# A two-layer hybrid encoder on one core: three seven-product pairs per unit, weights split in TensorE's order, gate weights cast by GpSimd

## The chip, the cores and the metric

The kernel runs on one core of a Trainium2 chip, as one launch. The metric is the device time of that launch in microseconds, as the median of several runs. The engines are named as the profile names them: PE is TensorE (matmuls; PEld its weight loads), DVE is VectorE, ACT is ScalarE, POOL is GpSimd, and SP's queue issues the loads from memory. The arithmetic is fp32, but TensorE takes each operand as a high part and a low part (both fp32r), so one product of two fp32 blocks is three matmuls: high by high, high by low, low by high.

## What is computed

256 tokens of width 2048 pass through two layers. Each layer is a token mixer and a gated feed-forward block, both with a residual and an RMS norm ahead:

```python
x = x + mixer(rms_norm(x, norm_mix[i]))
h = rms_norm(x, norm_ffn[i])
x = x + (silu(h @ w_gate) * (h @ w_up)) @ w_down     # 2048 -> 5632 -> 2048
```

Layer 0's mixer is grouped-query attention (16 query heads, 4 key heads of 128, norm and rotation on queries and keys). Layer 1's is a recurrent block: `h @ w_in` gives 2048 x-columns and 2048 gate columns; the x-columns go through a width-4 convolution and two gated linear recurrences, forward and backward, whose gates are block-diagonal products with 256 x 256 blocks; the sum times GeLU of the gate columns goes through `w_out`.

## The kernel before

All weights stream from memory once, in halves of 128 x 1024 fp32 (512 KB). `load_half` issues the load of one half into a buffer `raw`, ScalarE casts it to the high part `hi`, and VectorE subtracts to get the low part `lo`. Each of the three has five buffers. The halves are taken in the order of the list `order`, which is the order in which TensorE uses them. TensorE's own order is the order of the code. On the other engines a scheduler places the instructions by a timeline of its own, within the dependences; `follow(i, j)` adds the rule that i comes after j on its engine.

TensorE's stream also carries the small work of the mixers. `later(delay, fn)` puts a function on a list, `step()` is called between matmuls and counts, and when the count is reached the function is run at that place. `USUAL` and `LATE` give the delays of one attention head: the sums of squares, the scores, the turning of the probabilities, the values, and the split of the rotated query (`qs`). `WHEN` gives those of one block of the recurrence: four gates, four decays, four scans, GeLU, two finishes. In the projections of the recurrence a step is one `three`, that is three 256-wide matmuls; in attention's, one 512-wide and one 256-wide.

The feed-forward block works on units of 4 x 128 hidden columns, eleven in a layer. For one unit, the 16 contraction tiles are taken as 8 pairs. A pair holds two tiles of the gate weights and two of the up weights. Four accumulators (c11, c21, c12, c22: gate and up for each half of the tokens) take a plain pair as 8 products (`wide`). For the pairs named in `SEVEN` a Strassen-like form needs 7 products: `Norm.form` makes four sums of activations (`forms`) once per layer, `load_seven` makes four sums of the weights (t1 to t4) and splits them too, and four products go to banks of their own (m1, p5, p7, p6), which `unit` adds up at the end of the last such pair (lines 692 to 697). At a unit's end VectorE empties the four accumulators (L700, L703), the result is turned, split and kept as `act` tiles.

`PARTS` says after how many hidden tiles their share of `w_down` is multiplied: after the first unit of the next part come four down groups (512 output columns each) of the part before, all in a row. Each ends in `add_residual`. Accumulators are PSUM banks: four `acc` (`new_acc`) and four `pm`; before, down groups use `acc`.

## Time and profile before

| what | value |
|---|---|
| median of 3 runs | 2016.78 us (2014.33 to 2016.87) |
| profiled execution, its own time | 2015.84 us |
| its span, first to last instruction | 2013.9 us |
| mean granted TensorE clock | 0.997 |
| busy: PE / DVE / ACT / POOL | 1996.0 / 1527.1 / 1283.5 / 226.1 us |
| memory read | 382.13 MB, 191 GB/s over the span |
| attention | up to about 190 us, its output projection to 275 us |
| feed-forward of layer 0 | 275 to 978 us |
| recurrence | 978 to about 1230 us, its output projection to 1307 us |
| feed-forward of layer 1 | 1307 us to the end |

A row of the groups view names line, engine, operation, output and inputs by the program's tile names, shape and count, then busy time, mean ns of one, and the idle time of the engine just before with what ended it. A timeline row gives start, duration, engine, line, tiles and how many instructions were merged. A row of stretches gives, for each engine, the busy time and the number of instructions, then the granted clock, the DMA share and GB/s. The matmul time of one instruction is its latency; matmuls overlap, so pace is read from starts.

### The profile page before, as it was taken

Reading aid. Unit: us, or ns where it says so; the run is one execution under the profiler, and the core shown is the slowest. Engines: PE = TensorE matmul, PEld = TensorE weight load, DVE = VectorE, ACT = ScalarE, POOL = GpSimd, SP = SyncE. Lnnn points to the kernel's source line nnn. Section 1 sums busy time; section 2 is a strip of 40 time slices with the busy share of each in tenths; the row PEclk is TensorE's granted clock in tenths of the full one; section 3 lists DMA queues with packets and bytes.
Section 4 is the critical chain, followed back from the end, with each engine's and each line's share of the span. In section 5 each row is a group of like instructions: output and inputs, shape, how many; then the busy total and the mean of one; then the engine's idle time right before and its main releaser. Section 6 shows DMA issues by size and latency. Waiting matters only on the chain.

```text
span 2013.9 us, 27692 instructions
## 1 busy us (share of the span) xinstructions
PE 1996.0 (99%) x9994; PEld 1701.5 (84%) x9994; DVE 1527.1 (76%) x1982; ACT 1283.5 (64%) x1985; POOL 226.1 (11%) x305
## 2 busy tenths in 40 slices
PE   9999999999999999999899999999999999999999
PEld 8888888888888888888799998888888888888887
DVE  7888698886568865686768886898886578856764
ACT  7566676666346674467688987867665456654562
POOL 0454220000000000001333330400000000000000
PEclk9999999999999999999999999999999999999999
DMA  8444565655656656665656555565666556666654
GB/s 315 151 130 138 184 200 190 211 197 185 212 182 208 200 185 212 196 200 187 198 158 189 181 176 178 188 202 185 211 207 196 189 188 197 213 198 197 199 180 156
DMA packets 108569, 386.04 MB, mean 192 GB/s; under 512 B 12176, under 2 KB 12432, under 8 KB 108304
## 3 DMA queue, kind: packets, MB, share of 16 engines
q1 hardware_dynamic: 108288, 384.26, 59.0%
q8 instruction: 78, 1.28, 0.2%
q14 instruction: 59, 0.48, 0.1%
q10 hardware_dynamic: 144, 0.02, 0.0%
HBM read 382.13 MB, written 2.10 MB: 191 GB/s over the span
## 4 chain that ended last, share of the span: by engine, by line
PE 92%; DVE 4%; POOL 2%; issue 1%; DMA 1%; ACT 0%; SPq 0%; POOLq 0%; DVEq 0%; ACTq 0%
PE acc L261 24%; PE acc L258 24%; PE acc L259 24%; PE acc L238 3%; PE acc L239 3%; PE acc L240 3%; PE pm L259 2%; PE pm L258 2%; PE pm L261 2%; PE acc L227 2%; DVE lo L111 1%; POOL hb L508 1%; PE pm L240 1%; PE pm L239 1%; PE acc L225 1%
## 5 line engine op out<-in xcount | busy, mean ns | idle before, releaser
L111 DVE TENSOR_TENSOR lo<-raw,hi 128x1024 fp32r<-128x1024 f32 (+1 forms) x617 | 754.4, 1235 | 364.2 <-ACT hi L110 358.9
L110 ACT CAST hi<-raw 128x1024 fp32r<-128x1024 f32 (+1 forms) x617 | 639.3, 1049 | 535.1 <-PE acc L259 496.7
L258 PE MATMUL acc<-hi,xg 128*128 128x512 f32 x1100 | 427.9, 389 | 0.0
L259 PE MATMUL acc<-hi,xg 128*128 128x512 f32 x1100 | 427.9, 389 | 0.0
L261 PE MATMUL acc<-lo,xg 128*128 128x512 f32 x1100 | 427.9, 389 | 0.0
L258 PE MATMUL acc<-hi,act 128*128 128x512 f32 x960 | 373.9, 389 | 0.0
L261 PE MATMUL acc<-lo,act 128*128 128x512 f32 x960 | 373.5, 389 | 0.0
L259 PE MATMUL acc<-hi,act 128*128 128x512 f32 x960 | 373.5, 389 | 0.0
L258 PEld LDWEIGHTS acc<-hi,xg 128*128 128x128 f32 x1100 | 206.5, 188 | 42.9
L261 PEld LDWEIGHTS acc<-lo,xg 128*128 128x128 f32 x1100 | 206.5, 188 | 42.9
L259 PEld LDWEIGHTS acc<-hi,xg 128*128 128x128 f32 x1100 | 206.5, 188 | 42.9
L261 PEld LDWEIGHTS acc<-lo,act 128*128 128x128 f32 x960 | 180.2, 188 | 37.5
L259 PEld LDWEIGHTS acc<-hi,act 128*128 128x128 f32 x960 | 180.2, 188 | 37.4
L258 PEld LDWEIGHTS acc<-hi,act 128*128 128x128 f32 x960 | 180.2, 188 | 36.8
L348 ACT COPY hid<-turned 32x256 f32<-32x256 f32 x436 | 175.9, 404 | 10.2 <-DVE turned L341 5.3
L348 POOL COPY hid<-turned 32x256 f32<-32x256 f32 x84 | 58.3, 694 | 801.8 <-DVE turned L341 731.0
L239 PE MATMUL acc<-xg,hi 128*128 128x256 f32 x512 | 146.0, 285 | 1.4 <-DVE xg L363 1.4
L238 PE MATMUL acc<-xg,hi 128*128 128x256 f32 x512 | 146.3, 286 | 0.0
L240 PE MATMUL acc<-xg,lo 128*128 128x256 f32 x512 | 145.6, 284 | 0.0
L227 PE MATMUL acc<-xg,hi 128*128 128x512 f32 x384 | 125.9, 401 | 1.5 <-DVE xg L363 1.5
L131 ACT CAST wsh<-ws 128x1024 fp32r<-128x1024 f32 x88 | 92.2, 1050 | 43.3 <-DVE ws L126 43.2
L132 DVE TENSOR_TENSOR wsl<-ws,wsh 128x1024 fp32r<-128x1024 f32 x88 | 107.7, 1226 | 0.0
(216 smaller groups left out, 2655.3 us busy)
## 6 DMA issues: line engine op xcount, KB each, us to landing
raw<-in_w_gate_dram SPq DMA_DIRECT2D x176, 512.0 KB, 3.9
raw<-in_w_up_dram SPq DMA_DIRECT2D x176, 512.0 KB, 4.1
raw<-in_w_down_dram SPq DMA_DIRECT2D x176, 512.0 KB, 4.3
raw<-in_w_in_dram SPq DMA_DIRECT2D x64, 512.0 KB, 4.3
raw<-in_w_qv_dram SPq DMA_DIRECT2D x40, 512.0 KB, 4.0
raw<-in_w_o_dram SPq DMA_DIRECT2D x32, 512.0 KB, 3.5
raw<-in_w_out_dram SPq DMA_DIRECT2D x32, 512.0 KB, 3.6
graw<-in_w_gates_dram SPq DMA_DIRECT2D x32, 256.0 KB, 3.5
```

Source lines behind the costliest of these rows:

```text
L110: newest["cast"] = act.copy(hi[:, sl], raw[:, sl])
L111: dve.tensor_tensor(lo[:, sl], raw[:, sl], hi[:, sl].bitcast(F32), ALU.subtract)
L131: act.copy(hs[:, sl, :], sums[:, sl, :])
L132: dve.tensor_tensor(ls[:, sl, :], sums[:, sl, :], hs[:, sl, :].bitcast(F32), ALU.subtract)
L227: pe.matmul(acc, w, xs[k], start=(k == 0), stop=stop)
L238: pe.matmul(o, hi, x[:, :S], start=start, stop=False)
L239: pe.matmul(o, hi, x[:, S:], start=False, stop=False)
L240: pe.matmul(o, lo, x[:, :S], start=False, stop=stop)
L258: pe.matmul(o, xh, wh, start=start, stop=False)
L259: pe.matmul(o, xl, wh, start=False, stop=False)
L261: pe.matmul(o, xh, wl, start=False, stop=stop)
L348: (eng.copy if eng is act else eng.tensor_copy)(to[:, :, :, i, :], of[:, :, :, j, :])
```

## The change

1. `SEVEN` has three pairs (0, 3, 5) for nine of the eleven units; units 1 and 2 keep two (0, 5). The seven products are issued in another order: those with plain weights first.
2. `load_seven` casts, sums and splits in the order of the products, and `behind` ties each cast on ScalarE, and each sum or subtraction on VectorE, behind the last one of its kind. So weights are split in the order in which TensorE uses them, everywhere.
3. `parts` gives the split weights of the feed-forward parts two more buffers for `hi` and `lo` (seven in all); the sums of weights use buffers of the same ring.
4. `PARTS` is 8, 8, 8, 8, 12: after each unit from the third to the tenth come two down groups (`ffn_plan`), which now use the `pm` banks. `act` tiles have four buffers.
5. At the start of the recurrence `held` puts the casts from the fifth weight half on behind the last tile of the norm (`xg`), and the first block's gates come later (`WHEN_FIRST`).
6. In attention the first six heads' scores come later (`EARLY`), the last head's by three steps; VectorE scales the probabilities in place of GpSimd.
7. The gate weights are cast by GpSimd instead of ScalarE, from four raw buffers instead of two.

```diff
-PARTS = [16, 16, 12]
+PARTS = [8, 8, 8, 8, 12]
-SEVEN = (0, 4)
+SEVEN = (0, 3, 5)
+FEWER = (0, 5)
+FEW = (1, 2)
+RING = 5
+MORE = 2
-LATE = ((10, 23, 15, 13, 9), (5, 15, 17, 9, 5))
+EARLY = (32, 31, 30, 28, 26, 24)
+LATE = ((10, 23, 15, 13, 9), (5, 18, 17, 9, 5))
 WHEN = (18, 25, 32, 39, 42, 46, 50, 54, 58, 60, 62, 64, 66, 70, 74)
+WHEN_FIRST = (28, 34, 40, 46, 49, 53, 57, 60, 62, 64, 66, 68, 70, 74, 78)
...
+    def parts(shape):
+        n = ring[0] = (ring[0] + 1) % (RING + MORE)
+        if ft and n >= RING:
+            return [scope[-1].tile(shape, F32R, tag="x" + t, name=nm(t), bufs=MORE) for t in ("hi", "lo")]
+        return [wp.tile(shape, F32R, tag=t, name=nm(t), bufs=RING) for t in ("hi", "lo")]
+
+    def behind(key, i):
+        if key in newest:
+            follow(i, newest[key])
+        newest[key] = i
...
     def load_half(src, pieces=1, then=None):
...
-            newest["cast"] = act.copy(hi[:, sl], raw[:, sl])
-            dve.tensor_tensor(lo[:, sl], raw[:, sl], hi[:, sl].bitcast(F32), ALU.subtract)
+            behind("cast", act.copy(hi[:, sl], raw[:, sl]))
+            behind("rest", dve.tensor_tensor(lo[:, sl], raw[:, sl], hi[:, sl].bitcast(F32), ALU.subtract))
+        for rule in held:
+            rule[0] -= 1
+            if rule[0] < 0:
+                follow(newest[rule[1]], rule[2])
...
     def load_seven(srcs):
...
+        def two(src, names):
+            hi, lo = parts([P, 2, WIDE]) if len(names) > 1 else [tmp(t, (P, 1, WIDE), F32R) for t in ("ohi", "olo")]
+            behind("cast", act.copy(hi, src))
+            for j, name in enumerate(names):
+                got[name] = hi[:, j, :], lo[:, j, :]
+            return lambda: behind("rest", dve.tensor_tensor(lo, src, hi[:].bitcast(F32), ALU.subtract))
+
+        def add(o, x, y):
+            behind("rest", dve.tensor_tensor(o, x, y, ALU.add))
+
+        sums = [tmp("ws", (P, 2, WIDE)) for _ in range(2)]
+        (t1, t3), (t2, t4) = ([t[:, j, :] for j in range(2)] for t in sums)
+        two(raw[0], ("b11", "b21"))()
+        add(t1, b11, b12)
+        add(t3, b12, b22)
+        two(raw[1][:, 1:, :], ("b22",))()
+        first = two(sums[0], ("t1", "t3"))
+        add(t2, t1, b22)
+        add(t4, t2, b21)
+        second = two(sums[1], ("t2", "t4"))
+        first()
+        second()
...
+    def ffn_plan():
+        at = np.cumsum([0] + PARTS) // UNIT
+        plan = [("unit", i) for i in range(at[1])]
+        for p in range(len(PARTS) - 1):
+            for n, i in enumerate(range(at[p + 1], at[p + 2])):
+                plan.append(("unit", i))
+                plan += [("down", (p, g)) for g in range(2 * n, min(2 * n + 2, NW))]
+        return plan
...
+            if g == NW - 1 and self.g[0] == "norm_mix":
+                held.extend([[4, "cast", newest["xh"]], [4, "rest", newest["xl"]]])
...
+        if h < len(EARLY):
+            d_sc = EARLY[h]
...
-                eng.tensor_scalar(pr[:, a, :], pr[:, a, :], rs[:, a : a + 1], 1.0, ALU.mult, ALU.mult)
+                dve.tensor_scalar(pr[:, a, :], pr[:, a, :], rs[:, a : a + 1], None, ALU.mult)
...
-                for o, x, y in ((m1, a11, "b11"), (p5, n1, "t1"), (p7, n3, "t3"), (p6, n2, "t2")):
-                    product(o, x, wt[y], first, end)
-                for o, x, y in ((c21, a22, "t4"), (c11, a12, "b21"), (c12, n4, "b22")):
-                    product(o, x, wt[y], first, False)
+                for o, x, y in (
+                    (m1, a11, "b11"), (c11, a12, "b21"), (c12, n4, "b22"), (p5, n1, "t1"),
+                    (p7, n3, "t3"), (p6, n2, "t2"), (c21, a22, "t4"),
+                ):
+                    product(o, x, wt[y], first, end and any(o is m for m in (m1, p5, p7, p6)))
...
+                add_residual(i[1], wide_project(hid[i[0]], PARTS[i[0]], bank), None)
...
-        raw = tmp("graw", (P, 4, P), bufs=2)
+        raw = tmp("graw", (P, 4, P), bufs=GATE_BUFS)
...
-        act.copy(hi, raw)
+        pool.tensor_copy(hi, raw)
...
+        if b > 0:
+            held.clear()
...
-            when = WHEN if nxt else WHEN_LAST
+            when = WHEN_LAST if not nxt else WHEN if b else WHEN_FIRST
```

What this does to the order, at three places. First VectorE at the end of unit 0 of layer 0, before (e0 and e2 take accumulators c11 and c21, `hid` takes c12 and c22; the numbers are the tiles'):

```order
L128 TENSOR_TENSOR lo_748_3588<-raw_744_3584,hi_746_3586 128x512
L111 TENSOR_TENSOR lo_754_3629<-raw_752_3627,hi_753_3628 128x1024
L700 TENSOR_TENSOR e0_710_3428<-e0_710_3428,acc_670_3228 128x512
L700 TENSOR_TENSOR e2_712_3430<-e2_712_3430,acc_671_3229 128x512
L111 TENSOR_TENSOR lo_757_3647<-raw_755_3645,hi_756_3646 128x1024
L703 TENSOR_TENSOR hid_732_3545<-acc_672_3230,e1_711_3429 128x512
L703 TENSOR_TENSOR hid_732_3545<-acc_673_3231,e3_713_3431 128x512
```

and now, with the split of the next unit's first seven-product pair ahead of it (lo_764 to lo_770):

```order
L129 TENSOR_TENSOR lo_773_3661<-raw_771_3659,hi_772_3660 128x1024
L129 TENSOR_TENSOR lo_776_3679<-raw_774_3677,hi_775_3678 128x1024
L741 TENSOR_TENSOR e0_732_3493<-e0_732_3493,acc_674_3240 128x512
L741 TENSOR_TENSOR e2_734_3495<-e2_734_3495,acc_675_3241 128x512
L129 TENSOR_TENSOR lo_779_3697<-raw_777_3695,hi_778_3696 128x1024
L744 TENSOR_TENSOR hid_748_3574<-acc_676_3242,e1_733_3494 128x512
L744 TENSOR_TENSOR hid_748_3574<-acc_677_3243,e3_735_3496 128x512
```

One weight subtraction stands between the pairs of accumulators in both; now two more wide ones stand ahead of the first.

Second, VectorE where layer 0 ends and the recurrence begins, before (x is the residual, `hid` the turned copy, `xg` the scaled tiles of the norm):

```order
L282 TENSOR_TENSOR x_75<-x_75,acc_1717_8711 128x512
L111 TENSOR_TENSOR lo_1765_8946<-raw_1763_8944,hi_1764_8945 128x1024
L282 TENSOR_TENSOR x_75<-x_75,acc_1718_8712 128x512
L111 TENSOR_TENSOR lo_1790_9057<-raw_1788_9055,hi_1789_9056 128x1024
L341 STREAM_TRANSPOSE turned_1742_8837<-x_75 128x1024
L403 TENSOR_REDUCE nm_1739_8827<-ssq_665_3223 128x2
L348 COPY hid_1743_8838<-turned_1742_8837 32x8x32 x2
L408 TENSOR_SCALAR nm_1739_8827<-nm_1739_8827 128x2
L348 COPY hid_1743_8838<-turned_1742_8837 32x8x32 x6
L111 TENSOR_TENSOR lo_1793_9087<-raw_1791_9085,hi_1792_9086 128x1024
L111 TENSOR_TENSOR lo_1800_9130<-raw_1798_9128,hi_1799_9129 128x1024
```

and now:

```order
L129 TENSOR_TENSOR lo_1905_9155<-raw_1903_9153,hi_1904_9154 128x1024
L318 TENSOR_TENSOR x_75<-x_75,acc_1857_8920 128x512
L318 TENSOR_TENSOR x_75<-x_75,acc_1858_8921 128x512
L377 STREAM_TRANSPOSE turned_1882_9046<-x_75 128x1024
L443 TENSOR_REDUCE nm_1879_9036<-ssq_669_3235 128x2
L384 COPY hid_1883_9047<-turned_1882_9046 32x8x32 x2
L448 TENSOR_SCALAR nm_1879_9036<-nm_1879_9036 128x2
L384 COPY hid_1883_9047<-turned_1882_9046 32x8x32 x6
L466 TENSOR_TENSOR rsq_s_1881_9040<-nm_1879_9036,nr_1880_9039 128x2
```

The four weight subtractions between the residual and the norm's last tiles moved ahead of the residual or behind the tiles.

Third, VectorE after the first head's query is split in attention, before (hv is the mean square, mx the maximum of the scores, qs the split query) and now:

```order
L585 SCALAR_TENSOR_TENSOR hv2_159_855<-ms_139_758,ebt_104 128x2
L588 TENSOR_REDUCE mx_162_864<-pm_158_848 128x2
L313 CAST qs_151_822<-hq_149_816 128x256
L426 TENSOR_TENSOR rsq_s_161_858<-hv2_159_855,hf2_160_857 128x2
L314 TENSOR_TENSOR qs_151_822<-hq_149_816,qs_151_822 128x256
```

```order
L627 SCALAR_TENSOR_TENSOR hv2_162_883<-ms_139_758,ebt_104 128x2
L129 TENSOR_TENSOR lo_204_1042<-raw_202_1040,hi_203_1041 128x1024
L349 CAST qs_151_822<-hq_149_816 128x256
L466 TENSOR_TENSOR rsq_s_164_886<-hv2_162_883,hf2_163_885 128x2
L350 TENSOR_TENSOR qs_151_822<-hq_149_816,qs_151_822 128x256
L345 TENSOR_TENSOR hy_169_903<-acc_153_824,hy_169_903 128x256
L467 SCALAR_TENSOR_TENSOR rsq_s_164_886<-rsq_s_164_886,hf2_163_885 128x2
L630 TENSOR_REDUCE mx_165_892<-pm_161_876 128x2
```

The maximum of head 0's scores moved behind a weight subtraction and head 1's query.

## The prediction

> **What bounds the kernel now.** I read the page's busy row first, then the waits of TensorE, then stretches around each wait, and last the queues of the engines that feed it.

> ```profile
> PE 1996.0 (99%) x9994; PEld 1701.5 (84%) x9994; DVE 1527.1 (76%) x1982; ACT 1283.5 (64%) x1985; POOL 226.1 (11%) x305
> ```

> TensorE is busy for all but 18 us of the span. A busy PE need not be at full pace, so the pace comes from starts. Here are the first matmuls of the second unit of layer 0, with what VectorE did beside them:

> ```profile
> 317.36 0.39 PE L258 MATMUL pm<-hi,xg 128*128 128x512 f32 x1
> 317.59 0.39 PE L259 MATMUL pm<-hi,xg 128*128 128x512 f32 x1
> 317.59 1.21 DVE L111 TENSOR_TENSOR lo<-raw,hi 128x1024 fp32r<-128x1024 f32 x1
> ...
> 318.72 0.68 DVE L703 TENSOR_TENSOR hid<-acc,e 128x512 f32<-128x512 f32 x1
> ```

> The next unit begins at 359.52, 186 matmuls later: 42.16 / 186 = 0.2267 us for each 512-wide matmul. In the feed-forward parts (190 to 975 us, and from 1230) the waits of TensorE show nothing. All waits over 0.5 us lie in the mixers (columns: total us, times, longest):

> ```profile
> PE pm L240 <- DVE qs L314: 3.6, 2, 2.8
> PE pm L238 <- DVE xs L313: 2.8, 2, 1.7
> PE acc L227 <- DVE xg L363: 1.5, 1, 1.5
> PE pm L604 <- POOL pr L598: 1.5, 1, 1.5
> PE acc L239 <- DVE xg L363: 1.4, 1, 1.4
> ...
> PE pm L239 <- DVE xs L314: 1.0, 1, 1.0
> PE pm L416 <- POOL cb L739: 0.7, 1, 0.7
> ```

> (The xg wait of 1.5 is the start of the program and stays.) Stretches around them, the clock in the column after POOL:

> ```profile
> core 0: us, PE busy (x) PEld busy (x) DVE busy (x) ACT busy (x) POOL busy (x), PEclk, DMA share, GB/s
> 69.20:72.30 3.10, 0.28 (x3) 0.07 (x1) 3.10 (x5) 0.14 (x2) 2.83 (x3) 1.00 0.17 69
> 72.30:75.80 3.50, 3.49 (x13) 3.11 (x14) 3.21 (x10) 1.45 (x3) 1.34 (x2) 0.58 0.50 150
> 100.00:190.00 90.00, 89.26 (x562) 79.25 (x562) 80.31 (x177) 58.92 (x165) 49.94 (x63) 1.00 0.43 134
> 317.36:359.52 42.16, 42.16 (x187) 34.91 (x186) 37.27 (x43) 29.38 (x42) 0.00 (x0) 1.00 0.64 219
> 986.80:991.00 4.20, 2.10 (x13) 1.47 (x12) 3.75 (x11) 1.51 (x4) 0.23 (x4) 1.00 0.61 178
> 991.00:994.50 3.50, 3.50 (x19) 3.50 (x18) 1.38 (x2) 1.42 (x2) 0.00 (x0) 0.51 0.73 235
> 1001.10:1007.20 6.10, 2.15 (x9) 1.24 (x8) 6.05 (x11) 2.13 (x3) 3.06 (x4) 0.79 0.83 256
> 1007.20:1011.20 4.00, 4.00 (x20) 4.00 (x20) 1.20 (x3) 2.38 (x4) 1.52 (x3) 0.50 0.43 131
> 1020.00:1230.00 210.00, 210.00 (x1720) 208.26 (x1720) 171.02 (x282) 188.73 (x321) 74.11 (x93) 1.00 0.56 172
> ```

> A wait is followed here by about 3.5 to 4 us at half clock, so it costs twice. In all three places VectorE is the full engine. So: fewer matmuls pay in full while VectorE keeps up, and the waits in the mixers are a second, separate reserve.

> **Part 1, matmuls.** A seven-product pair replaces 8 products by 7, three matmuls each. Nine of eleven units per layer get a third pair (units 1 and 2 keep two): 18 pairs, 54 matmuls, 54 x 0.2267 = 12.2 us.

> **Part 2, what VectorE and ScalarE pay.**

> ```profile
> L131 ACT CAST wsh<-ws 128x1024 fp32r<-128x1024 f32 x88 | 92.2, 1050 | 43.3 <-DVE ws L126 43.2
> ...
> L126 DVE TENSOR_TENSOR ws<-ws,raw 128x512 f32<-128x512 f32 x88 | 60.8, 691 | 0.6
> ```

> ```profile
> 304.83 0.69 DVE L126 TENSOR_TENSOR ws<-raw,raw 128x512 f32<-128x512 f32 x1 [3.42 <-DMA raw<-in_w_up_dram]
> ...
> 308.38 2.35 DVE L111 TENSOR_TENSOR lo<-raw,hi 128x1024 fp32r<-128x1024 f32 x2
> ```

> Back to back, a 1024-wide subtraction takes 1.14 us (2.35 - 1.21), a 512-wide one about 0.61 (0.69 less the same 0.08 of overlap). A plain pair costs VectorE two wide subtractions; a seven-product pair three wide ones, one narrow and four sums: 4.2 us more. A two-pair unit keeps VectorE busy for 37.27 of 42.16 us, so one with three needs 41.5, against 183 x 0.2267 = 41.5 for TensorE. Alone that is no slack at all. But the new order puts two down groups (48 matmuls, 10.9 us, each; VectorE 4 x 1.14 + 2 x 0.65 = 5.9) after every unit from the third to the tenth: 53.3 of 63.3 us. Only unit 0 and the last have three pairs without them, and unit 0's successor has two. ScalarE gets two casts more per pair (about 1.6 us net on 29.38). Cost on the path: none, covered by this slack and by seven buffers of split weights instead of five; the 3.42 us that VectorE idled before a sum, for a DMA, also show room. Nothing more is loaded, and the loads keep TensorE's order on SP's queue, five deep as before; there the cover is the lead of the splitting over TensorE. The forms of the third pair (one set per layer, on ScalarE, GpSimd and VectorE) are made while the output projection's last group still runs. Four tiles for the hidden values instead of five cost nothing: the fifth unit writes over the first one's, whose last reader, the fourth down group, stands before it.

> The new product order does add a wait: bank c12 is written after two products (1.36 us) instead of six (4.1 us). VectorE empties it behind one weight subtraction, as the order still has it. In the rows above that ended at 318.72 + 0.68 = 319.40, 2.04 us into the unit: 0.7 us late. Units 0 to 1 and 1 to 2 follow directly in each layer; from the third on a down group stands between and uses the other banks. In before the later boundaries emptied the bank in time, so I charge one per layer, 1.4 us. Ends: 0, and 2 x (0.7 + 4.2 + half of 3.5 at half clock) = 13.

> **Part 3, attention.**

> ```profile
> 69.08 0.28 PE L238 MATMUL pm<-kv,qs 128*128 128x256 f32 x1
> ...
> 71.31 0.94 DVE L314 TENSOR_TENSOR qs<-hq,qs 128x256 fp32r<-128x256 f32 x1
> ...
> 73.05 0.69 DVE L585 SCALAR_TENSOR_TENSOR hv<-ms,ebt 128x2 f32<-128x2 f32 x1
> ```

> ```profile
> L598 POOL TENSOR_SCALAR pr<-pr,rs x30: 480/482/493, 78.4 to 190.8; 128x256 f32<-128x256 f32 x30
> ...
> L598 DVE TENSOR_SCALAR pr<-pr,rs x2: 349/351/353, 195.1 to 195.3; 128x256 f32<-128x256 f32 x2
> ```

> Head 0's scores come 10 steps later; a step is one 512 and one 256-wide matmul, 0.35 us, so they start at 72.6, when qs is ready (72.25). That wait and its slow clock go: 2.8 + 3.5 x 0.42 = 4.3 us. The wait of 1.5 for the scaled probabilities (1.8 with its tail) goes, since GpSimd no longer scales them behind the rotations; the last head's 0.7 goes with three steps more. Together 6.8. Given back: VectorE's queue now has a weight subtraction and head 1's query split ahead of head 0's maximum, and a second subtraction behind it. From 73.05 that queue, both exponentials and the scaling add up to about 8.1 us, to 81.2; TensorE wants the turn 17 steps and a set of scores after 73.3, at 80.1. Take 1.1 lost. Later heads: VectorE was busy for 80.31 of 90 us in 100 to 190 (the stretches above), and 11 heads with 0.7 us more make 88, so this cover is thin; it holds since GpSimd, 1 us freer per head, slows VectorE less. Net 5.7; ends 2 (the wait turns into as long a one) and 6.8.

> **Part 4, start of the recurrence.**

> ```profile
> 978.32 0.28 PE L238 MATMUL acc<-xg,hi 128*128 128x256 f32 x1
> 978.44 0.28 PE L239 MATMUL acc<-xg,hi 128*128 128x256 f32 x1
> ...
> 981.32 1.24 DVE L341 STREAM_TRANSPOSE turned<-x 128x1024 f32<-128x1024 f32 x1
> ...
> 985.83 2.36 DVE L111 TENSOR_TENSOR lo<-raw,hi 128x1024 fp32r<-128x1024 f32 x2
> ...
> 988.37 0.48 DVE L363 SCALAR_TENSOR_TENSOR xg<-hid,pk,xg 128x256 fp32r<-128x256 f32 x1
> ```

> What is lost: 986.8 to 991, 4.2 less 13 matmuls of 0.12, 2.7; then 3.5 x 0.49 = 1.7; 1001.1 to 1007.2, 6.1 less 9 x 0.12, 5.0; then 2.0. Together 11.4. The new rule holds the casts from the fifth weight half on behind the last xg. In the new order two weight subtractions no longer stand between the residual and its transpose, nor two between the copies and xg: about 1.5 + 2.3 us earlier, so the last xg come near 984.5 to 986.2, and the thirteenth is wanted at 987: 4.4 gone. The first gates come 10 steps of three matmuls (3.6 us) later, but counted from an earlier point. VectorE's conv work now stands between weight subtractions that wait for buffers TensorE frees. The last of them needs one freed 20.6 us after 978.3; with cast (1.05), subtraction (1.14) and the split behind (0.43) that is 23.4, and TensorE wants it at 22.5. So about 0.9 stays of 7.0. Net 10.5; ends 4.4 (as late as now) and 11.4.

> **Part 5, gate weights on GpSimd.**

> ```profile
> L770 POOL TENSOR_TENSOR glo<-graw,ghi 128x512 fp32r<-128x512 f32 x32 | 49.4, 1544 | 37.5 <-ACT ghi L769 37.5
> ...
> L769 ACT CAST ghi<-graw 128x512 fp32r<-128x512 f32 x32 | 19.6, 612 | 17.3 <-PE pm L239 10.0 <-DMA graw<-in_w_gates_dram 6.0 <-PE acc L239 1.4
> ```

> ```profile
> 69.33 2.64 POOL L508 TENSOR_TENSOR hb<-hy,rope 64x256 f32<-64x256 f32 x2 [1.08 <-DVE hy L309]
> ```

> ScalarE loses 19.6 us in a stage where it is busy for 188.73 of 210. GpSimd gets 32 casts; no row has that cast, the nearest (482 ns for 256 wide) gives 0.96 us, the subtraction at 1.54 an upper end: 31 to 49 us, room beside 74.11 of 210. The gate loads stay on SP's queue behind weight loads; with four raw buffers instead of two they wait less. Behind a cast that waits for a DMA stand GpSimd's products for the scans, due only at the block's end. Cost on the path 0; from -1 (a freer ScalarE) to +5.
> VectorE and GpSimd slow each other: at 69.65 a subtraction took 1.74 us beside GpSimd's 2.64. [...]

> **Sum.** -12.2 + 1.4 - 5.7 - 10.5 + 0 = -27.0. The profiled execution took 2015.84 (span 2013.9 and 1.9 around it), so 1988.8; the median of the runs is 0.94 higher: 1989.7, say 1990.

> **Rivals.**
> 1. The mixers' waits only move: matmuls fall, but conv and scores stay late, since VectorE was busy for all of 69.2 to 72.3 and 6.05 of 6.10 us at 1001. Net 12.2 - 1.4 + 2 + 4.4 = 17, so 2000; with nothing from the mixers, 2006. For it: full VectorE. Against: the order frees it just ahead of xg, and more steps are given. Chance 0.15.
> 2. GpSimd holds VectorE: 31 us more in the recurrence, 171 to about 199 of 210; seven blocks each 4 us later could show as 1 us of wait and its slow clock at each, about 14 us: 2004. Against: it still fits. Chance 0.07.
> 3. Slower: a three-pair unit makes TensorE wait at its start, for its third and fourth bank (the second down group's sums stand behind weight subtractions) or for weights. Decides from 27 / 18 = 1.5 us per unit; at 1.4 us of wait and 1.5 of slow clock, 18 x 2.9 = 52: 2042. Against: that bank is wanted 3.4 us into the unit and freed about 1.9 in. Chance 0.05. [...]
> 4. My forecast, 1985 to 1997: 0.70. Else (a small gain or none): 0.03.

> **Range.** All gains in full: 12.2 + 6.8 + 11.4 = 30.4, 1986 against the median; I put 1985. The upper end, 2003, takes in most of rival 1 and 2. Faster by over 0.2% (4 us, about what these runs can tell from none) 0.92, within 0.02, slower 0.06.

> **What would show it.** PE records fewer by 54 and a unit of 41.5 us; no PE wait in the feed-forward over 1 us, except on c12 at two unit boundaries; the waits on xg and qs gone, one near 80 us on pr, one near 1001 on xs below 2 us; no stretch at half clock after 20 us or one short one. Wrong would be: half clock at unit starts, VectorE over 95% in 1020 to 1230 with PE idle, or the xs wait as long as before.

## The result, and the profile after

The changed kernel takes 2000.99 us (median of 4 runs, 1999.41 to 2001.07) against 2016.78 before (4 runs): ratio 0.9923, 95% interval 0.9906 to 0.994. The gain is 15.8 us where 27 were forecast. The time lies in the range that the prediction stated, 1985 to 2003, but outside the likeliest case's own range (1985 to 1997), and 1 us from the 2000 that the first rival gave. The profiled execution took 2001.05 us, its span is 1999.3, 14.6 shorter than before.

The busy row of the page:

```profile
PE 1981.1 (99%) x9940; PEld 1686.6 (84%) x9940; DVE 1629.9 (82%) x2154; ACT 1297.6 (65%) x1995; POOL 256.4 (13%) x315
```

TensorE has exactly 54 records fewer (9994 to 9940) and is busy for 14.9 us less; VectorE gained 102.8 us of work. The waits of TensorE, longest sums first:

```profile
PE pm L275 <- DVE pT L649: 3.6, 7, 0.9
PE pm L646 <- DVE pr L640: 2.5, 5, 0.9
PE acc L263 <- DVE xg L399: 1.9, 1, 1.9
PE acc L294 <- DVE e L741: 1.4, 2, 1.1
PE pm L275 <- DVE xs L350: 1.3, 2, 0.9
PE pm L274 <- DVE xs L349: 1.0, 1, 1.0
```

The waits of before on qs (2.8) and on xg in the recurrence (1.4) are gone. In their place stand twelve small ones in the attention: seven on pT, which is the transposed probabilities' low half that VectorE writes, and five on pr, which VectorE now scales. To see what each stage won, take the first matmul of each from the timeline of TensorE (start, duration, line, form); of after first, then of before (whose recurrence begins at 978.32, in a row of the prediction):

```profile
48.94 0.27 PE L590 MATMUL pm<-ident,hy 128*128 128x128 f32 x1
277.73 0.39 PE L294 MATMUL pm<-hi,xg 128*128 128x512 f32 x1
976.79 0.28 PE L274 MATMUL acc<-xg,hi 128*128 128x256 f32 x1
1296.65 0.39 PE L294 MATMUL pm<-hi,xg 128*128 128x512 f32 x1
```

```profile
47.43 0.28 PE L550 MATMUL pm<-ident,hy 128*128 128x128 f32 x1
275.20 0.39 PE L258 MATMUL pm<-hi,xg 128*128 128x512 f32 x1
...
1306.91 0.39 PE L258 MATMUL pm<-hi,xg 128*128 128x512 f32 x1
```

The differences of these starts are the lengths of the stages; the last stage ends with TensorE's last matmul, at 2010.19 before and 1995.54 after.

| stage | before | after | change | predicted |
|---|---|---|---|---|
| program's start, to the first turned head | 47.43 | 48.94 | +1.5 | 0 |
| attention, to the first feed-forward unit | 227.77 | 228.79 | +1.0 | -5.7 |
| feed-forward 0 | 703.12 | 699.06 | -4.1 | -5.4 |
| recurrence and its output projection | 328.59 | 319.86 | -8.7 | -10.5 |
| feed-forward 1 | 703.28 | 698.89 | -4.4 | -5.4 |
| sum | | | -14.7 | -27.0 |

Four places miss their sum, the attention by more than half of it. Stretches of after (columns as in the prediction; the clock stands after POOL), the first at the program's start:

```profile
7.00:10.50 3.50, 3.50 (x12) 3.07 (x13) 3.04 (x6) 3.30 (x8) 0.00 (x0) 0.54 1.03 416
100.00:190.00 90.00, 86.15 (x540) 75.63 (x539) 82.82 (x193) 55.24 (x159) 39.33 (x40) 1.00 0.39 124
1020.00:1230.00 210.00, 210.00 (x1679) 206.48 (x1679) 179.07 (x295) 178.49 (x293) 98.60 (x110) 1.00 0.56 173
```

In 100 to 190 TensorE was busy for 89.26 of 90 us before and is for 86.15 now, while VectorE went from 80.31 to 82.82, although the program advanced less in that time (540 matmuls instead of 562). The start's 1.5 us is no part of the change: TensorE's first wait, 1.9 us here and 1.5 in before, is followed here by a stretch at clock 0.54, and in a second profile of the same kernel (c1, below) by none.

What the attention's small waits look like, on three engines in order of time (rows are left out at the dots); a row's bracket gives the idle time before it and its releaser:

```profile
125.49 0.68 DVE L649 TENSOR_TENSOR pT<-pm,pT 128x512 fp32r<-128x512 f32 x1
...
126.23 0.39 PE L275 MATMUL pm<-pT,kv 128*128 128x256 f32 x1 [0.88 <-DVE pT L649]
...
126.72 2.41 POOL L548 TENSOR_TENSOR hb<-hy,rope 64x256 f32<-64x256 f32 x2 [3.01 <-DVE hf L468]
126.76 1.78 DVE L129 TENSOR_TENSOR lo<-raw,hi 128x1024 fp32r<-128x1024 f32 x1
...
129.21 0.73 POOL L549 TENSOR_TENSOR hq<-hy,rope 128x256 f32<-128x256 f32 x1
129.41 1.48 DVE L640 TENSOR_SCALAR pr<-pr,rs 128x256 f32<-128x256 f32 x2
130.23 0.30 PE L646 MATMUL pm<-ident,pr 128*128 128x128 f32 x1 [0.71 <-DVE pr L640]
```

VectorE goes from one instruction to the next with hardly a pause, in the rows left out too. The two scalings, 0.35 us each in the median of all 32, take 1.48 together here, beside GpSimd's products for hq. TensorE waits for pT and for pr because VectorE reaches them late.

### The profile page after: what moved, and what is told of

Its sections match the earlier page's. It is cut to its first block, busy times and chain, and to the rows that moved or that the text cites. A ratio compares the mean times of both kernels' runs of the same rounds, so it can differ in the third digit from the quotient of the medians.

```text
span 1999.3 us, 27804 instructions
## 1 busy us (share of the span) xinstructions
PE 1981.1 (99%) x9940; PEld 1686.6 (84%) x9940; DVE 1629.9 (82%) x2154; ACT 1297.6 (65%) x1995; POOL 256.4 (13%) x315
## 4 chain that ended last, share of the span: by engine, by line
PE 87%; DVE 7%; POOL 2%; issue 1%; ACT 1%; DMA 1%; SPq 0%; DVEq 0%; ACTq 0%; POOLq 0%
PE acc L294 16%; PE acc L295 16%; PE acc L297 16%; PE pm L297 8%; PE pm L295 8%; PE pm L294 8%; PE acc L274 3%; PE acc L275 3%; PE acc L276 3%; DVE lo L129 2%; PE acc L263 1%; POOL hb L548 1%; PE pm L275 1%; PE pm L276 1%; PE pm L274 1%
## 5 line engine op out<-in xcount | busy, mean ns | idle before, releaser
L129 DVE TENSOR_TENSOR lo<-raw,hi 128x1024 fp32r<-128x1024 f32 (+1 forms) x581 | 712.0, 1242 | 170.2 <-ACT hi L128 167.0
L128 ACT CAST hi<-raw 128x1024 fp32r<-128x1024 f32 (+1 forms) x581 | 596.6, 1048 | 299.1 <-PE acc L295 227.5
L294 PE MATMUL acc<-hi,xg 128*128 128x512 f32 x1036 | 403.3, 389 | 1.8 <-DVE e L741 1.4
L297 PE MATMUL acc<-lo,xg 128*128 128x512 f32 x1036 | 403.0, 389 | 0.0
L295 PE MATMUL acc<-hi,xg 128*128 128x512 f32 x1036 | 403.0, 389 | 0.0
L146 ACT CAST hi<-ws 128x1024 fp32r<-128x1024 f32 x124 | 130.6, 1054 | 194.5 <-DVE ws L152 192.3
L294 PEld LDWEIGHTS acc<-hi,xg 128*128 128x128 f32 x1036 | 194.5, 188 | 43.2 <-DVE e L741 2.3
L294 PE MATMUL pm<-hi,act 128*128 128x512 f32 x512 | 199.2, 389 | 0.0
L295 PE MATMUL pm<-hi,act 128*128 128x512 f32 x512 | 199.2, 389 | 0.0
L297 PE MATMUL pm<-lo,act 128*128 128x512 f32 x512 | 199.2, 389 | 0.0
L384 ACT COPY hid<-turned 32x256 f32<-32x256 f32 x436 | 175.9, 404 | 23.9 <-DVE turned L377 14.7
L294 PE MATMUL acc<-hi,act 128*128 128x512 f32 x448 | 174.6, 390 | 0.0
L297 PE MATMUL acc<-lo,act 128*128 128x512 f32 x448 | 174.4, 389 | 0.0
L295 PE MATMUL acc<-hi,act 128*128 128x512 f32 x448 | 174.3, 389 | 0.0
L149 DVE TENSOR_TENSOR lo<-ws,hi 128x1024 fp32r<-128x1024 f32 x124 | 151.8, 1225 | 6.4 <-ACT hi L146 3.6
```

The costliest lines, as they stand in the source:

```text
L128: behind("cast", act.copy(hi[:, sl], raw[:, sl]))
L129: behind("rest", dve.tensor_tensor(lo[:, sl], raw[:, sl], hi[:, sl].bitcast(F32), ALU.subtract))
L146: behind("cast", act.copy(hi, src))
L149: return lambda: behind("rest", dve.tensor_tensor(lo, src, hi[:].bitcast(F32), ALU.subtract))
L294: pe.matmul(o, xh, wh, start=start, stop=False)
L295: pe.matmul(o, xl, wh, start=False, stop=False)
```

## The experiments

Each is an edit of the changed kernel. Two profiles of the changed kernel agree in each stage to 0.2 us, but for the start with its clock (the changed kernel again, below); times of one kernel spread over 0.5 to 5.5 us, so stages are read first. No run takes away the two additional buffers, the new `PARTS` or the order of the splits alone, so what each of these is worth by itself is not shown.

**Scaling back on GpSimd.**

```diff
-                dve.tensor_scalar(pr[:, a, :], pr[:, a, :], rs[:, a : a + 1], None, ALU.mult)
+                eng.tensor_scalar(pr[:, a, :], pr[:, a, :], rs[:, a : a + 1], 1.0, ALU.mult, ALU.mult)
```

> The changed kernel with one line undone: GpSimd scales the probabilities again, the scores keep their new steps. In the changed kernel TensorE loses 0.35 to 1.1 us at nearly every head between 80 and 195 us, mostly on pT and pr from VectorE. Theory (VectorE is full there because of the 0.7 us of scaling per head): the small waits on pT go, the part from 100 us to the first feed-forward matmul (277.73) shortens by 3 to 4 us, the wait for pr near 80 is about 1 us longer since GpSimd scales behind the next head's rotation; in all 1997 to 1999. Rival (the earlier places of the first six scores crowd VectorE, not the scaling): the waits on pT stay, 2000 to 2002.

Measured: 1996.95 us (ratio to before 0.9903, 0.989 to 0.9917). The attention takes 225.59 us instead of 228.79: 3.2 less. Its stretch and its waits from 75 to 200 us:

```profile
100.00:190.00 90.00, 88.43 (x554) 77.98 (x554) 77.07 (x175) 58.17 (x165) 50.87 (x64) 1.00 0.41 133
```

```profile
PE pm L646 <- POOL pr L640: 2.7, 3, 1.1
PE pm L275 <- DVE pT L649: 1.1, 3, 0.5
```

VectorE falls from 82.82 to 77.07 us, TensorE gains 2.3, the waits on pT fall from 3.6 to 1.1, and the wait for pr near 80 grows, as the theory had it. The time holds more than the edit: in this profile the start is without half clock (1.00 from 7.00 to 10.50 us; 1.6 us less), and the start of the recurrence has one (0.50 from 997.30 to 1000.30 us; 2.7 us more).

**Scaling on ScalarE.**

```diff
-                dve.tensor_scalar(pr[:, a, :], pr[:, a, :], rs[:, a : a + 1], None, ALU.mult)
+                act.activation(pr[:, a, :], pr[:, a, :], AF.Copy, scale=rs[:, a : a + 1])
```

> The changed kernel with the probabilities scaled by ScalarE (a copy with a scale, two of about 0.35 us per head), which is busy for 51 of 84 us there. Theory (VectorE is full because of the scaling): the waits on pT go, 3 to 5 us: 1996 to 1998. Rival (it is the chain of a head, not VectorE's load, or ScalarE's queue now stands behind the reciprocal and its weight casts come late): 2000 or more.

Measured: 1998.38 us (0.9911, 0.9897 to 0.9924); attention 226.19 us, 2.6 less. Whichever engine takes the scaling away from VectorE, the waits on pT shrink (here to 2.0). So it is VectorE's load, not the chain through GpSimd. ScalarE's copy takes 0.50 us, not the 0.35 that the expectation set.

**Steps of before for the scores.**

```diff
-EARLY = (32, 31, 30, 28, 26, 24)
+EARLY = ()
-LATE = ((10, 23, 15, 13, 9), (5, 18, 17, 9, 5))
+LATE = ((10, 23, 15, 13, 9), (5, 15, 17, 9, 5))
```

> The changed kernel with the steps of all scores as before (the first six heads again at 22, the last at 15); VectorE still scales the probabilities. Theory (VectorE is full because of the scaling): the waits on pT per head stay, and the wait of 2.8 us on qs with its half clock comes back, 4.3 us: first feed-forward matmul at 281 to 282, 2005. Rival (the new steps crowd VectorE): the waits per head go and only the qs wait comes back: feed-forward at 277 to 278, 2000 to 2001.

Measured: 2003.86 us (0.9934, 0.9921 to 0.9948); attention 230.62 us, 1.8 more than in the changed kernel. The wait of 2.8 on qs is back, but this time no half clock follows it:

```profile
72.30:75.80 3.50, 2.08 (x13) 1.91 (x14) 3.50 (x7) 0.58 (x3) 2.68 (x3) 1.00 0.42 140
```

The waits on pT fall from 3.6 to 2.4. Both theories have a part: the new steps remove a wait of 2.8 us, and crowd VectorE a little more. They are worth 1.8 us here, not the 4.3 of the prediction; the 1.5 us of half clock that followed this wait in before would come on top.

**The seven products in the old order.**

```diff
-                    (m1, a11, "b11"), (c11, a12, "b21"), (c12, n4, "b22"), (p5, n1, "t1"),
-                    (p7, n3, "t3"), (p6, n2, "t2"), (c21, a22, "t4"),
+                    (m1, a11, "b11"), (p5, n1, "t1"), (p7, n3, "t3"), (p6, n2, "t2"),
+                    (c21, a22, "t4"), (c11, a12, "b21"), (c12, n4, "b22"),
```

> The changed kernel with the seven products in the order of before (all four PSUM banks of the mixed products first, then c21, c11, c12). In the changed kernel TensorE waits at the second unit of each layer, 1.3 and 1.5 us, for bank c11, which the second product writes and VectorE still empties behind two weight subtractions. Theory (the early use of c11 alone makes these waits): both go, unit 0 to unit 1 without a gap, 2.8 us less: 1998. Rival (VectorE is behind at this place, and whatever comes second waits): the gap stays near 1 us, on another bank or on a weight, 2000 to 2001.

Measured: 2018.68 us (1.001, 1.0001 to 1.0019). Both theories fall: all that the change gained is gone again. The waits at 320 and 1339 are gone too, but each of the eight units that follow two down groups, in either layer, has a wait of 1.03 us; the feed-forward stages take 708.06 and 707.70 us. Its rows, in one of these units, which begins at 426.57:

```profile
428.47 0.40 PE L297 MATMUL pm<-lo,fh 128*128 128x512 f32 x1
428.90 0.68 DVE L318 TENSOR_TENSOR x<-x,pm 128x512 f32<-128x512 f32 x1
429.73 0.47 PE L294 MATMUL pm<-hi,fh 128*128 128x512 f32 x1 [0.86 <-DVE x L318]
```

The fourth product wants the bank that the second down group used, and VectorE adds that bank to the residual only at 428.90, behind weight subtractions. (At 11 of these 16 units the profile names a cast on ScalarE that ends as late, in its place. That cast is of a later pair's weights, and the addition stands there too, ending 0.15 us ahead of TensorE's start in all 16.) In the changed kernel the same bank is wanted sixth:

```profile
427.35 0.39 PE L294 MATMUL pm<-hi,xg 128*128 128x512 f32 x1
429.70 0.68 DVE L318 TENSOR_TENSOR x<-x,pm 128x512 f32<-128x512 f32 x1
430.75 0.39 PE L294 MATMUL pm<-hi,fh 128*128 128x512 f32 x1
```

It is free 3.0 us into the unit (430.38 less 427.35) and wanted at 3.4.

**The new order everywhere but in the second unit.**

```diff
+                if direct and first:
+                    prods = tuple(prods[j] for j in (0, 3, 4, 5, 1, 2, 6))
...
-                hid[int(np.searchsorted(ends, i, "right"))] += unit(FEWER if i in FEW else SEVEN)
+                hid[int(np.searchsorted(ends, i, "right"))] += unit(FEWER if i in FEW else SEVEN, i == 1)
```

> The changed kernel with the first pair of unit 1 alone in another order (the four PSUM banks of the mixed products first, then c11, c12, c21); all other units as changed. Theory (c11 is wanted too early only where a unit follows another at once, the other banks only where a down group stands between): the waits of 1.2 to 1.3 us at 320 and of 1.5 at 1339 go and nothing comes in their place: both feed-forward stages 1.3 to 1.5 us shorter, 1998.2. Rival (in unit 1 the weights of the mixed products come late, as in the kernel with this order everywhere): a wait of about 1 us in the first 4 us of unit 1, 2000 to 2001.

Measured: feed-forward 697.91 and 697.83 us, 1.15 and 1.06 less; the waits named e are gone. That is the theory, a little under its size: in layer 1 a wait of 0.4 us on the next accumulator (`hid`) comes in their place. The time is 2001.32 (0.9918, 0.9905 to 0.9932), no better, since here 2.7 us went at the start of the recurrence, after the same waits on xs as in the changed kernel: there the clock fell this time (0.50 from 1000.30 to 1003.30 us).

**Three pairs in every unit.**

```diff
-FEW = (1, 2)
+FEW = ()
```

> The changed kernel with three seven-product pairs in units 1 and 2 too: 4 pairs and 12 matmuls fewer, 2.7 us if VectorE keeps up. These two units follow each other with no down group between, where the prediction reckoned 41.5 us of VectorE work in 41.5 us: no slack. Theory (the lead of seven buffers and the down groups carry it): feed-forward stages 1.3 to 1.4 us shorter each (697.7 and 697.5), 1998.3. Rival (without slack a unit starts late): a new wait of 1 us or more at the start of unit 2 or 3 in each layer, on a bank or a weight, 2001 to 2004.

Measured: 2004.58 us (0.9938, 0.9926 to 0.9951). Twelve matmuls less, and the feed-forward stages are longer, 700.62 and 699.79. The rival holds in its main point, that without slack TensorE waits, but most of the wait is elsewhere. At the start of the third unit of each layer the third product waits 0.9 us for an accumulator. Twice as much, 1.9 us with its tails, is lost in the middle of that unit; in layer 0:

```profile
374.40 6.64 ACT L384 COPY hid<-turned 32x256 f32<-32x256 f32 x16 [0.62 <-DVE turned L377]
381.06 1.04 ACT L146 CAST hi<-ws 128x1024 fp32r<-128x1024 f32 x1
382.14 1.22 DVE L149 TENSOR_TENSOR lo<-ws,hi 128x1024 fp32r<-128x1024 f32 x1 [5.34 <-ACT hi L146]
382.16 0.50 PE L294 MATMUL pm<-hi,fh 128*128 128x512 f32 x1 [0.84 <-ACT hi L146]
```

The sums' cast stands on ScalarE behind 16 copies of the transposed hidden values; VectorE idles for 5.34 us.

**Start of the recurrence as before.**

```diff
-                held.extend([[4, "cast", newest["xh"]], [4, "rest", newest["xl"]]])
+                pass
...
-            when = WHEN_LAST if not nxt else WHEN if b else WHEN_FIRST
+            when = WHEN_LAST if not nxt else WHEN
```

> The changed kernel without the rule that holds the casts behind the last xg, and with the gates at their old steps: what the prediction counted as 10.5 us of gain in the recurrence and the profile shows as 8.7. Theory (both together made it): the waits on xg near 10 us into the recurrence and on xs near 25 us into it come back with their half clock; the stage is 328 to 329 us again and the time 2009 to 2010. Rival (the order of weights made by ScalarE and VectorE, or freed ScalarE, made much of it): 2003 to 2006.

Measured: 2006.12 us (0.9948, 0.9935 to 0.996); the stage takes 326.19 us, 6.3 more than in the changed kernel and 2.4 less than before.

```profile
PE pm L274 <- DVE xs L349: 3.2, 2, 2.9
PE pm L275 <- DVE xs L350: 1.5, 1, 1.5
PE pm L456 <- POOL cb L777: 0.8, 1, 0.8
PE acc L275 <- DVE xg L399: 0.7, 1, 0.7
```

So both rules make most of the 8.7, in between the two expectations; the rest goes to the order in which VectorE and ScalarE now make the weights, which alone halves the wait on xg (1.4 before). Part of the 6.3 is clock: 6.8 us at half clock lie among and behind the waits on xs in this profile, and none in the changed kernel's.

**Without the rule that holds the casts**, the first of those two edits alone.

> The changed kernel without the rule that holds the casts, the first block's gates at their new, later steps. Theory (the two halves are separate): the waits on xg come back, 2.7 us and some 1.7 of half clock, the waits on xs stay as in the changed kernel: 2004 to 2006. Rival (VectorE's work is only moved to the place where xs is made): the xg waits come back and the xs waits go, 2001.

Measured: 2002.40 us (0.993, 0.9917 to 0.9942), stage 322.80. The waits on xg and cb are back (0.7 and 0.8), those on xs fall to one of 1.8. Neither expectation is met whole. Most of what the rule saves at xg, VectorE loses at xs; of its own worth, 2.9 us in these two profiles, about half can be clock: here 3.4 us at half clock follow the wait on xs, in the changed kernel none (below). The later gates, 326.19 less 322.80, are worth 3.4.

**Later gates.**

```diff
-WHEN_FIRST = (28, 34, 40, 46, 49, 53, 57, 60, 62, 64, 66, 68, 70, 74, 78)
+WHEN_FIRST = (36, 40, 44, 48, 51, 53, 57, 60, 62, 64, 66, 68, 70, 74, 78)
```

> The changed kernel with the first recurrence block's four gate steps at 36, 40, 44, 48 instead of 28, 34, 40, 46. In the changed kernel TensorE waits there on xs for 1.2, 0.65 and 1.0 us, and in four of the other profiles a stretch at half clock follows. Theory (the gates stand too early by about 3 us, eight steps): the xs waits fall below 0.5 us in sum, no half clock, the stretch from the first recurrence matmul to the second feed-forward is 317 us (319.9 in the changed kernel's profile, up to 323.6 in the others): 1997 to 1998. Rival (VectorE is behind there as a whole and the wait moves to later work of the block): a new wait of 2 us or more between 1003 and 1020, 2000 to 2001.

Measured: 1998.97 us (0.9906, 0.9893 to 0.992), stage 318.18, 1.7 less. One wait on xs is left, 0.9 us, and no other came; nearer to the theory, short of its 317.

**Gate weights cast by ScalarE.**

```diff
-        pool.tensor_copy(hi, raw)
+        act.copy(hi, raw)
```

> The changed kernel with the 32 gate-weight casts on ScalarE again. Theory (they lie beside TensorE's work on either engine): the recurrence keeps its length, TensorE has no wait in 1020 to 1230, 2000 to 2001. Rival (GpSimd's casts hold VectorE up): VectorE's busy time in 1020 to 1230 falls by 10 us or more and the start of the recurrence loses less, 1998.

Measured: 1999.14 us (0.9912, 0.9899 to 0.9926), stage 319.31; its start was one without half clock (1.00 from 7.00 to 10.50 us), which is 1.6 of the 1.9 us to the changed kernel.

```profile
1020.00:1230.00 210.00, 210.00 (x1671) 206.10 (x1670) 175.83 (x290) 189.34 (x316) 69.06 (x86) 1.00 0.56 173
```

TensorE is busy throughout in both kernels. With the casts GpSimd is busy for 29.5 us more in this stretch (98.60 less 69.06), and VectorE for 3.2, a tenth of that, with five instructions more (295 and 290).

**The changed kernel again.**

> The changed kernel itself once more, for what differs between two profiles of the same program. Theory (a wait of about 2 us switches the clock, and small differences of the loads decide it): the program's first wait is again between 1.1 and 2.3 us, with 3 us of half clock behind it only if it exceeds 2.0, worth 1.5 us; the waits on xs are 2.8 to 4.5 us again, with or without half clock. Rival (the kernel always has a slow start): half clock from 7 to 11 us whatever the wait.

Measured: 2001.26 us (0.9923, 0.9909 to 0.9937). Stages as in the first profile to 0.2 us, but for the start: 47.98 instead of 48.94 for the first turned head, no half clock behind a first wait that ended 1.85 us after the last matmul's start, against 2.17. The rival is out.

**Combined.** Four edits: GpSimd scales; the first head's turn seven steps later; the second unit's order; later gates.

> The changed kernel with four edits: GpSimd scales the probabilities, the first head's turn stands 7 steps later (24 instead of 17), unit 1 starts in the other product order, the first block's gates stand later. Theory (the four waits are separate): 3.2 us from the scaling, up to 2.5 from the first turn, 2.8 from the two units, 2.8 from the gates: 1990 to 1992, where the prediction had put the change itself. Rival (VectorE's work in the mixers only comes late at the next place): 1995 or more.

Measured: 1993.33 us (0.988, 0.9867 to 0.9894), the fastest kernel here, some 8 us under the changed one. Attention 225.48, feed-forward 698.29 and 697.85, recurrence 318.23. Scaling, second unit and gates keep most of their gains. The later turn gave nothing (225.59 without it): the wait for pr was only moved.

```profile
PE pm L648 <- POOL pr L642: 2.9, 2, 1.5
```

## Why the prediction was right in kind and too large in size

**Matmuls.** Right: 54 fewer, at full price. 27 x 0.2267 = 6.1 us per layer, of which 4.1 and 4.4 show; the rest is the bank waits of the next paragraph.

**Bank wait.** Its place was right, the unit that follows another at once, but not the bank and the size. In layer 0 c11 waits, not c12. The new order writes c11 second, 0.68 us into the unit, and VectorE empties it behind two weight subtractions, not one:

```profile
318.81 2.35 DVE L129 TENSOR_TENSOR lo<-raw,hi 128x1024 fp32r<-128x1024 f32 x2
321.07 1.28 DVE L741 TENSOR_TENSOR e<-e,acc 128x512 f32<-128x512 f32 x2
321.81 0.50 PE L294 MATMUL acc<-hi,xg 128*128 128x512 f32 x1 [1.13 <-DVE e L741]
```

In layer 1 c11 waits for only 0.5 us, and the third product, which writes c12, for 1.0 more:

```profile
1340.28 0.69 DVE L741 TENSOR_TENSOR e<-e,acc 128x512 f32<-128x512 f32 x1
...
1341.11 0.48 PE L294 MATMUL acc<-ohi,fh 128*128 128x512 f32 x1 [0.86 <-ACT hi L128]
```

It starts 0.14 us after VectorE has emptied the second accumulator, c21. The profile names a cast that ends at about the same time; that the emptied bank is the one waited for is inferred from the times. With a wait of 0.5 us at the first unit of layer 0 it all comes to 3.7 us instead of 1.4 (gaps between the starts of neighbours beyond 0.2267 us, summed over both stages). Only the boundary of units 0 and 1 shows it.
What the prediction did not price is the other side of this order. It treated it as a cost; the old order costs 17.7 us once down groups use the mixed products' banks. Rival 3 named the place and gave its margin as 3.4 less 1.9; it is 0.4.

**No slack with three pairs.** Right as a statement on units 1 and 2, though two thirds of the loss come by ScalarE's queue, beside which VectorE idles, and not by VectorE's total.

**Attention.** This step failed. The gain at qs came (2.8 and its half clock), and the loss near 80 us was put well (1.1, measured 1.1 and 0.9 behind it). The wrong sentence is that the thin cover "holds since GpSimd, 1 us freer per head, slows VectorE less". 0.7 us more per head, at 80.31 of 90 us, was not covered: TensorE's waits from 75 to 200 us, now all on pT and pr, sum to 6.1 us instead of 2.2 (1.5 on pr, in a row of the prediction, and 0.7 on qs). With the tails behind them, counted as starts later than the usual pace of each shape, TensorE lost 5.5 us up to 76 us and 6.3 from there to 202 in before, and loses 1.0 and 11.7 now. VectorE, at 89% on average in before (80.31 of 90 us), was full there in places: busy for 6.88 of 7 us from 105 to 112 us, and for 5.97 of the next 7. With 0.7 us per head taken off VectorE again, by GpSimd or by ScalarE, 3.2 or 2.6 us come back. GpSimd's rotation still ran beside VectorE, and the scalings took up to 0.90 us each there.
This is rival 1 for the attention, which put the net at +2 to the good; it was 1.0 to the bad.

**Recurrence.** The mechanism was right and the remainder too small: waits on xs of 2.3 by the profile, with their tails 2.8, instead of 0.9. The prediction had seen that conv work would stand between weight subtractions; the last xs half stands behind one here. It ends 25.4 us into the stage, where the prediction had 23.4, and the subtraction's 1.2 us is a part of that:

```profile
1000.28 0.41 DVE L350 TENSOR_TENSOR xs<-xc,xs 128x256 fp32r<-128x256 f32 x1
1000.62 1.21 DVE L129 TENSOR_TENSOR lo<-raw,hi 128x1024 fp32r<-128x1024 f32 x1
1001.75 0.41 DVE L350 TENSOR_TENSOR xs<-xc,xs 128x256 fp32r<-128x256 f32 x1
```

The 8.7 us of this stage hold some luck. In four other profiles with the same three waits (scaling on GpSimd, scaling on ScalarE, the second unit's order, three pairs everywhere) half clock follows them, and the stage takes 321.26 to 322.64 us; in the two profiles of the changed kernel none does, and it takes 319.86 and 320.03. With that clock the change would have gained 6.0 to 7.3 us here.

**Half clock.** The prediction took half clock behind a long wait for granted. That was too simple: the wait of 2.8 us on qs has it in before and has none in the run with the steps of before, and the waits on xs have it in some profiles only. The last section says what the traces show of this.

**Gate casts.** Right, 0 on the path. Rival 2, which charged VectorE every microsecond of GpSimd, is out by a factor of ten; that VectorE pays for each of them was the author's assumption, and no run shows it. From 1020 to 1230 us a wide subtraction takes 1.327 us in the mean with GpSimd's casts (62 of them) and 1.323 in before (57). What the rival left out is who comes second. GpSimd's product for h, before and after, each with the weight subtraction beside it:

```profile
1068.53 0.75 POOL L823 TENSOR_TENSOR h<-h,h 128x256 f32<-128x256 f32 x1 [3.39 <-DVE h L822]
1068.62 1.73 DVE L111 TENSOR_TENSOR lo<-raw,hi 128x1024 fp32r<-128x1024 f32 x1
```

```profile
1056.17 1.20 DVE L129 TENSOR_TENSOR lo<-raw,hi 128x1024 fp32r<-128x1024 f32 x1
1056.34 1.63 POOL L861 TENSOR_TENSOR h<-h,h 128x256 f32<-128x256 f32 x1 [2.14 <-DVE h L860]
```

In both pairs the one that starts second is longer, by 0.5 us behind GpSimd's 0.75 and by 0.9 behind VectorE's 1.20; the first keeps its time (1.22 us for a subtraction with no GpSimd beside it, at 428.56 in the changed kernel; 0.74 for a product, the median of the 14 of before). In the changed kernel 13 of the 14 products start during a subtraction and take 1.63 to 1.64 us; the last one, and all 14 of before, start during a 256-wide instruction of VectorE and take 0.74 to 0.75. Of the 110 instructions of GpSimd that start between 1020 and 1230 us, 91 start while one of VectorE runs, 24 of them during a weight subtraction. The rival's error was to let VectorE pay each time.

**The sum.** Missing of 27.0: 6.7 in the attention, 2.3 in the feed-forward, 1.8 in the recurrence, 1.5 from the clock at the start. The time lies in the stated range only because its upper end took in the first two rivals.

## What to carry to other kernels

VectorE, free for a tenth of a stage (busy for 80.31 of 90 us), had no cover to give to work of 0.7 us that recurs with every head: ask which queue such work stands in at the moment its result is due, and give it to an engine with more room (GpSimd was busy for 39.33 of the 90 us here, ScalarE for 55.24; 3.2 and 2.6 us came back). When a new place for one piece of work (the down groups) and a new order of another (the products) come together, price each without the other; an order that looks like a small cost can be what makes the rest possible. Read such changes by stages, since the clock after a wait moved whole times by 1.5 to 2.7 us here.

## What was not expected of the hardware

The length of a wait alone does not decide here whether TensorE's clock falls: the 2.8 us on qs were followed by half clock in before (0.58 from 72.30 to 75.80 us) and by none with the steps of before (1.00). At the program's start, from the start of the last preparing matmul to that of the next, 1.82 and 2.01 us (two kernels) left it at full speed; 2.08, 2.17, 2.30 and 2.32 halved it for 3.4 us. (In the run with later gates the first matmuls came at about half the pace after only 1.57 us, 11 from 7.00 to 10.50 us where before has 20. There the trace's record of the clock begins, at full, only at 10.23 us, and in before at 4.56, so this need not be a fall.) In the recurrence the three waits of 1.2, 0.65 and 1.0 us within 3.5 us were followed by half clock in four profiles, and in the two of the changed kernel by none.

```profile
994.05:997.46 3.41, 1.73 (x11) 1.15 (x9) 3.41 (x7) 1.65 (x3) 1.51 (x3) 1.00 0.76 243
997.46:1004.29 6.83, 6.20 (x29) 6.20 (x30) 3.75 (x9) 3.70 (x7) 2.14 (x4) 0.50 0.70 238
```

```profile
997.18:1000.59 3.41, 2.16 (x17) 1.78 (x15) 3.41 (x7) 1.39 (x2) 2.38 (x6) 1.00 0.86 272
1000.59:1004.00 3.41, 2.40 (x18) 2.20 (x19) 3.24 (x7) 2.02 (x4) 0.61 (x3) 1.00 0.95 278
```

With ScalarE's scaling TensorE is busy for 1.73 us of the step, so 1.7 us of waiting lie in it; in the changed kernel a boundary divides the waiting into 1.3 and 1.0 us. Over all 14 profiles, each fall in the recurrence came behind a step with at most 2.00 us of busy TensorE, and none behind one with 2.15 or more. So after the same waits the fall went, in these profiles, with where the boundary lay, and it moved a time by some 2.7 us. The busy time of a row is not the exact measure: in the attention no fall came behind steps with 1.78 us (the combined kernel) and 1.84 us (the steps of before). No wait here is as long as a step (the longest is 2.9 us, on xs with the recurrence's start as before): a step in which TensorE was partly busy was enough. What exactly is counted within a step stays open.
